# Full 128x128 array tiles for the low key products, the low value products and the meta transposes of a FoX attention

## The chip, the cores and the metric

The kernel runs on one core of one Trainium2 chip, in one launch. The metric is the device time of an execution in microseconds (us). Before the change the median of three runs is 858.16 us (857.74 to 858.84).

## The reference, cut to what matters

One layer of a streaming encoder: a gated linear attention (GLA) and a softmax attention with forget gates (FoX) work on the same normed tokens (512 prompt frames, 16 meta tokens ahead of them, 32 frames of a running stream), and a feed-forward stage follows. The change touches the FoX attention of the prompt, 8 heads of width 64:

```python
def _fox_attend(q, k, v, cq, ck, qpos, kpos):
    s = jnp.einsum('bhqd,bhkd->bhqk', q, k) * (FOX_DH ** -0.5)
    s = s + cq[..., :, None] - ck[..., None, :]           # running sums of log forget gates
    s = jnp.where(kpos[None, :] <= qpos[:, None], s, NEG)
    p = jax.nn.softmax(s, axis=-1)
    return jnp.einsum('bhqk,bhkd->bhqd', p, v)
```

It is called per query block of 128 with all 528 keys (16 meta, 512 prompt); the outputs include the new keys and values, and all of it is float32.

## The kernel before, in words

Every large product is made of three products of split numbers: hi(a)hi(b) + hi(a)lo(b) + lo(a)hi(b), where hi is the value rounded to the matmul type fp32r by ScalarE (ACT) and lo the rest, by VectorE (DVE). A product on TensorE (PE) is a weight load (PEld) of up to 128x128 numbers and a matmul that streams up to 512 columns past them. In the forms of the profile "128\*128" is the array tile: partitions of the contraction \* columns of the weights. "64\*128" uses half of the array's rows, "128\*64" and "128\*16" only some of its columns.

The tokens' projections are computed in units of 128 weight columns: one DMA of 512 KB (`wr`), times the norm's gain on GpSimd (POOL, line 223), split into `wh` and `wl`, then 48 products. In the attention stage, roughly 135 to 295 us of the profiled execution, the small products of the heads stand between these projections as in a zip: `attend()` yields after each small step, and `fill()` then emits 8 products (`GAP_HEAD`) of the next unit in `FILL`: keys (`fk`), queries (`fq`) of a pair of heads, and gates (`ga`, `gb`). The engines run their queues in that order, set at build time.

For each pair of heads `p`, `proj_fk(p)` (line 748) computes the keys `kT` and splits them: `kh` (hi of one head's keys) stands on both halves of the partitions, the second half by a copy on DVE (line 767); lo of both heads goes into columns 1024 to 1551 of the tile `pq`, each head on its own half (line 768). `proj_fq(p)` (line 794) puts into `pq` the queries of each head: hi on the head's own half, lo on the other. So one 128-row product of queries and `kh` gives q·hi(k), and a second one, with the 64 rows of the head's own half, adds hi(q)·lo(k).

`head_scores(h)` (line 902) makes the scores of one head in four query blocks. Its pieces have 144, 272, 400 and 400 + 128 key columns; each is a product with `kh`, one with lo(k), and, but for the first part of the last block, one bf16 product with `mask_b`, all into one PSUM bank. DVE then adds the forget sums and takes the minimum (line 820), ACT takes the exponential (825), DVE normalizes (827, 828). `head_values(h)` (line 924) transposes the probabilities on PE: the 16 meta columns of each query block into `ps_ptm` (line 930), the rest into `ps_pt` (line 940), splits them into `pth` and `ptl`, and multiplies with V. V's tile holds hi(v) in 64 columns and lo(v) in the next 64, so the product with `pth` gives both parts; the one with `ptl` takes the hi columns alone (line 957). The two halves of the result are added at lines 961 and 962.

Of the kernel before, what the change touches and what calls it, by code (L numbers as in the profile page):

```python
# [29 lines left out]
# Token columns: [meta 16 | meta again 16 (unused) | sample 32 | prompt 512].  # L30
TOK = 576
M0 = 32              # first column of the tokens whose outputs are needed
# [6 lines left out]
# Column offsets in w_in.  # L39
GQ, GK, GV, GR, GLR, FQ, FK, FV, FF, GA, GB = 0, 256, 512, 1024, 1536, 1552, 2064, 2576, 3088, 3096, 4120  # L40

# Key columns of the FoX keys: [meta 16 | prompt 512].
KP = META            # first prompt key
# [4 lines left out]
def tile_hybrid_step(  # L48
# [50 lines left out]
    def after(ins, earlier):  # L99
        """order on one engine's queue only"""  # L100
        for e in earlier:
            tc.add_manual_dep(ins, e.name, mybir.DependencyInfo(mybir.DependencyClass.NoSync,
                                                                mybir.DependencyReason.DATA), reason="table")
# [7 lines left out]
    def split_lo(out, in_, hi, eng=None):  # L111
        (eng or DVE).tensor_tensor(out, in_, hi.bitcast(F32), ALU.subtract)  # L112

    # how many products of the projections stand between two steps of a chain of small ones
    GAP_RB, GAP_GATE, GAP_DECAY, GAP_STATE, GAP_OUT, GAP_HEAD, GAP_LEAD = 8, 7, 4, 16, 12, 8, 18

# [9 lines left out]
    # rows 0..16: hi, 32..48: lo, 64..80: hi  # L126
# [23 lines left out]
    # the tensor engine's clock rises with use: some products while the first loads are under way  # L150
# [17 lines left out]
    # suf[t', t] = 1 where t' > t in the same chunk; ind[t', c] = 1 where t' is in chunk c  # L168
    # (ind with zeros on both sides)
# [122 lines left out]
    # hi(x) and lo(x) of the first 64 tokens side by side  # L292
# [27 lines left out]
    def newton(out, y, ms, n, w, name):  # L320
        """out = y * (1.5 - 0.5 * ms * y * y)"""
        a = small([w], name + "_a")
        DVE.tensor_tensor(a[:n], y[:n], y[:n], ALU.mult)
        DVE.scalar_tensor_tensor(a[:n], a[:n], -0.5, ms[:n], ALU.mult, ALU.mult)
        DVE.scalar_tensor_tensor(out, a[:n], 1.5, y[:n], ALU.add, ALU.mult)

    def rsqrt(out, sumsq, n, w, name):
        """out = (sumsq / D + EPS) ** -0.5"""
        ms = small([w], name + "_ms")
        DVE.tensor_scalar(ms[:n], sumsq, 1.0 / D, EPS, ALU.mult, ALU.add)  # L330
        y = small([w], name + "_y")
        ACT.activation(y[:n], ms[:n], AF.Ln)
        ACT.activation(y[:n], y[:n], AF.Exp, scale=-0.5)
        newton(out, y, ms, n, w, name)
# [12 lines left out]
    def token_tile(wh, wl, N, t, ps, kstep=KD):  # L347
        c0, n = TT[t]
        i = 0
        if t == 0:  # L350
            # hi(x) on the first half of the partitions, lo(x) on the second
            for b, k in [(b, k) for k0 in range(0, KD, kstep) for b in (wh, wl) for k in range(k0, k0 + kstep)]:
                mm(ps[:, :N], x2[k // 4][:, k % 4, :], b(k), i == 0, i == 2 * KD - 1)
                i += 1
                yield
            return
        for a, b, k in [(a, b, k) for k0 in range(0, KD, kstep) for a, b in ((xh, wh), (xl, wh), (xh, wl))
                        for k in range(k0, k0 + kstep)]:
            mm(ps[:n, :N], a[:, k, c0: c0 + n], b(k), i == 0, i == 3 * KD - 1)
            i += 1  # L360
            yield
# [75 lines left out]
    # r broadcast over the partitions: rb[p, token] = r[token]  # L437
# [45 lines left out]
    def blocks_steps(key, ks, wh, wl, ah, al, spans, evac, psf, both=False):  # L483
        """out[columns of the weights, tokens]; ah/al(k, a, b) give the moving operand."""
        last = ks[-1]
        pss_ = [psf(f"ps_{key}_{ci}") for ci in range(len(spans))] if both else None
        todo = [(ci, part) for part in (0, 1) for ci in range(len(spans))] if both else \
               [(ci, part) for ci in range(len(spans)) for part in (0, 1)]
        for ci, part in todo:
            a, b = spans[ci]  # L490
            if not both and part == 0:
                ps = psf(f"ps_{key}_{ci}")
            if both:
                ps = pss_[ci]
            i = 0
            for w_, x_ in ((wh, ah), (wl, ah), (wh, al)):
                for k in ks:
                    if (k == last) == bool(part):
                        mm(ps[:, : b - a], w_[:, k, :], x_(k, a, b), part == 0 and i == 0, part == 1 and i == 2)
                        i += 1  # L500
                        yield
            if part:
                evac(ci, a, b, ps[:, : b - a])
# [125 lines left out]
    def evac_fv(t, n, ps):  # L629
# [12 lines left out]
        for g in range(2):  # L642
            src = v[:, 256 * g: 256 * g + 256].rearrange("t (h d) -> t h d", h=4)
            if t == 0:
                # rows 0..15: [hi | lo] against hi(P); rows 32..47: [hi | 0] against lo(P)
                DVE.memset(vt[g].bitcast(F32)[0:48], 0.0)
                ACT.activation(vt[g][0:META, :, 0:64], src[0:META], AF.Copy)
                ACT.activation(vt[g][32:32 + META, :, 0:64], src[0:META], AF.Copy)
                DVE.tensor_tensor(vt[g][0:META, :, 64:128], src[0:META], vt[g][0:META, :, 0:64].bitcast(F32),
                                  ALU.subtract)  # L650
            else:
                ACT.activation(vt[g][:, :, 0:64], src, AF.Copy)
                DVE.tensor_tensor(vt[g][:, :, 64:128], src, vt[g][:, :, 0:64].bitcast(F32), ALU.subtract)
# [6 lines left out]
    # gq into block-diagonal form: per chunk [head 0 tokens | head 1 tokens]  # L660
# [42 lines left out]
    t2 = [blk([TM], F32, f"t2_{hh}", "t2") for hh in range(GH)]  # L703

    def gla_out_steps(name, w, pv, products, dsts):
        """dsts: (tile AP, view of a PSUM-shaped AP) pairs."""
# [37 lines left out]
    kT, pq, kk_, qq_ = [None] * 4, [None] * 4, [None] * 4, [None] * 4  # L744
# [3 lines left out]
    def proj_fk(p):  # L748
# [11 lines left out]
        # hi(k) of a head on both halves of the partitions; lo(k) of both heads  # L760
        pq[p] = ppool.tile([P, PTW], F32R, tag="pt", name=f"pq{p}")
        kk_[p] = [blk([META + SEQ], F32R, f"kh{p}_{hh}") for hh in range(2)]
        for hh in range(2):
# [4 lines left out]
            split_lo(pq[p][own, 1024:1552], k_[own, :], kh[own])  # L768
# [25 lines left out]
    def proj_fq(p):  # L794
# [8 lines left out]
        # hi(q) of a head on its own half of the partitions, lo(q) on the other half  # L803
# [12 lines left out]
    def score_min(sb, a, pv, cb, m, name):  # L816
        """-scores + mask (PSUM) + running sum of log forgets -> sb; running minimum"""
# [30 lines left out]
    def sample_scores(g):  # L848
        """4 heads x 32 queries on the partitions"""
# [44 lines left out]
    # column of (key tile j, query tile i) is 384 j + 128 i  # L894
# [7 lines left out]
    def head_scores(h):  # L902
        p, b0 = h // 2, 64 * (h % 2)
# [3 lines left out]
        for i in range(4):  # L907
            w = META + P * (i + 1)
            q_ = qq_[p][h % 2][:, P * i: P * i + P]
            kh, kl = kk_[p][h % 2], pq[p][b0: b0 + 64, 1024:1552]  # L910
            sb = sbt[:, SBO[i]: SBO[i + 1]]
            m = 3.0e38
            for a, b in ([(0, w)] if i < 3 else [(0, 400), (400, 528)]):
                ps = pss(f"ps_s{h}_{i}_{a}")
                mm(ps[:, 0: b - a], q_, kh[:, a:b], True, False)
                mm(ps[:, 0: b - a], q_[b0: b0 + 64], kl[:, a:b], False, b < w)
# [7 lines left out]
    def head_values(h):  # L924
# [4 lines left out]
        for i in range(4):  # L929
            TE.transpose(pm[:META, P * i: P * i + P], sbt[:, SBO[i]: SBO[i] + META], ident)  # L930
# [24 lines left out]
        for j in range(4):  # L955
            a = 512 * j
            mm(po[0:64, P * j:], V[j + 1][g][:, hh, 0:64], ptl[:, a: a + SEQ - P * j], False, j == 3)
# [92 lines left out]
    # GLA output gate  # L1050
# [68 lines left out]
    # the table of Ln and Exp, back after the last sigmoid  # L1119
# [15 lines left out]
    def final_part(g, tiles, late=None):  # L1135
        """late: what is still to be added to the last block of hs"""
# [18 lines left out]
    def final_early():  # L1155
        """mean of the squares of all but the last block, + EPS"""
# [115 lines left out]
```

## Time and profile before

| | us |
|---|---|
| median of three runs | 858.16 |
| span of the profiled execution, first to last instruction | 855.3 |
| what lies around the span, by the median | 2.9 |
| PE busy, whole span | 837.9 |
| DVE busy, whole span | 450.2 |
| PE busy from 155 to 204 us | 49.0 of 49.0 |
| DVE busy from 204 to 214 us | 9.0 of 10.0 |

PE is busy 98% of the span. But a matmul counts as busy until its modelled end, and matmuls overlap: whether PE could go faster is read from the distance between the starts of consecutive products, not from the busy share. The timeline merges consecutive instructions of one kind into a row with a count (x7). Its second number is from the first one's start to the last one's end.

### The profile page before, as it was taken

Reading aid. Unit: us, or ns where it says so; the run is one execution under the profiler, and the core shown is the slowest. Engines: PE = TensorE matmul, PEld = TensorE weight load, DVE = VectorE, ACT = ScalarE, POOL = GpSimd, SP = SyncE. Lnnn points to the kernel's source line nnn. Section 1 sums busy time; section 2 is a strip of 40 time slices with the busy share of each in tenths; the row PEclk is TensorE's granted clock in tenths of the full one; section 3 lists DMA queues with packets and bytes.
Section 4 is the critical chain, followed back from the end, with each engine's and each line's share of the span. In section 5 each row is a group of like instructions: output and inputs, shape, how many; then the busy total and the mean of one; then the engine's idle time right before and its main releaser. Section 6 shows DMA issues by size and latency. Waiting matters only on the chain.

```text
span 855.3 us, 14966 instructions
## 1 busy us (share of the span) xinstructions
PE 837.9 (98%) x6279; PEld 797.2 (93%) x6279; DVE 450.2 (53%) x828; ACT 311.5 (36%) x567; POOL 159.7 (19%) x162
## 2 busy tenths in 40 slices
PE   8999999999999999999999999999999999999996
PEld 7877898888888999999999999999999999999996
DVE  6765347777657655367576644422333444433434
ACT  6760454454434633222223343411112343411323
POOL 4315111131111376023553000011110000000000
PEclk9997999999999999999999999999999999999999
DMA  8612213421422123323223233223323233223212
GB/s 240 172 49 73 50 43 101 120 77 50 121 57 80 50 74 99 90 84 88 86 79 95 78 95 94 80 74 100 99 77 97 82 91 97 77 74 100 88 37 105
DMA packets 132788, 75.37 MB, mean 88 GB/s; under 512 B 14032, under 2 KB 128000, under 8 KB 132720
## 3 DMA queue, kind: packets, MB, share of 16 engines
q1 hardware_dynamic: 131680, 72.27, 29.7%
q0 software_dynamic: 1024, 2.14, 1.1%
q8 instruction: 49, 0.80, 0.4%
q14 instruction: 19, 0.16, 0.1%
q10 hardware_dynamic: 16, 0.00, 0.0%
HBM read 69.57 MB, written 4.83 MB: 87 GB/s over the span
## 4 chain that ended last, share of the span: by engine, by line
PE 85%; DVE 4%; DMA 3%; POOL 3%; ACT 3%; issue 2%; SPq 0%; ACTq 0%; POOLq 0%; DVEq 0%
PE ps_dn L106 23%; PE ps_up L106 22%; PE ps_ga L106 5%; PE ps_gb L106 5%; PE ps_wo L106 5%; PE ps_fv L106 3%; PE ps_fk L106 3%; PE ps_ya L106 3%; PE ps_yb L106 2%; PE ps_s L106 2%; PE ps_fq L106 2%; DMA wr<-in_w_in_dram 1%; PE ps_pv L106 1%; PE ps_g L106 1%; DVE wl L112 1%
## 5 line engine op out<-in xcount | busy, mean ns | idle before, releaser
L109 ACT ACTIVATE wh<-wr 128x1024 fp32r<-128x1024 f32 x110 | 116.2, 1056 | 273.5 <-PE ps_dn L106 133.2
L112 DVE TENSOR_TENSOR wl<-wr,wh 128x1024 fp32r<-128x1024 f32 x110 | 150.5, 1368 | 99.9 <-ACT wh L109 99.7
L223 POOL TENSOR_TENSOR wr<-wr,gmix 128x1024 f32<-128x1024 f32 x30 | 58.2, 1943 | 149.4 <-DMA wr<-in_w_in_dram 143.1
L106 PE MATMUL ps_up<-xl,wh 128*128 128x256 f32 (+1 forms) x512 | 85.0, 288 | 0.0
L106 PE MATMUL ps_up<-xh,wh 128*128 128x256 f32 (+1 forms) x512 | 85.0, 288 | 0.0
L106 PE MATMUL ps_up<-xh,wl 128*128 128x256 f32 (+1 forms) x512 | 84.9, 288 | 0.0
L106 PE MATMUL ps_dn<-uh,wl 128*128 128x256 f32 (+1 forms) x512 | 80.0, 288 | 0.0
L106 PE MATMUL ps_dn<-uh,wh 128*128 128x256 f32 (+1 forms) x512 | 80.0, 288 | 0.0
L106 PE MATMUL ps_dn<-ul,wh 128*128 128x256 f32 (+1 forms) x512 | 79.7, 287 | 0.0
L1188 DVE SCALAR_TENSOR_TENSOR u<-ps_up,u 128x288 f32<-128x288 f32 x64 | 28.1, 441 | 85.0 <-ACT u L1187 85.0
L106 PEld LDWEIGHTS ps_up<-xh,wh 128*128 128x128 f32 x512 | 72.3, 188 | 0.1
L106 PEld LDWEIGHTS ps_up<-xl,wh 128*128 128x128 f32 x512 | 72.2, 188 | 0.0
L106 PEld LDWEIGHTS ps_up<-xh,wl 128*128 128x128 f32 x512 | 72.0, 188 | 0.0
L106 PEld LDWEIGHTS ps_dn<-uh,wh 128*128 128x128 f32 x512 | 70.5, 188 | 0.0
L106 PEld LDWEIGHTS ps_dn<-uh,wl 128*128 128x128 f32 x512 | 70.2, 188 | 0.0
L106 PEld LDWEIGHTS ps_dn<-ul,wh 128*128 128x128 f32 x512 | 70.0, 188 | 0.0
L1187 ACT ACTIVATE u<-ps_up 128x288 f32<-128x288 f32 x64 | 25.4, 398 | 120.9 <-PE ps_up L106 120.9
L1227 DVE TENSOR_TENSOR dt<-ps_dn,fin 128x288 f32<-128x288 f32 (+1 forms) x32 | 14.1, 441 | 64.2 <-PE ps_dn L106 64.2
L1229 POOL TENSOR_TENSOR xres<-xres,dt 128x288 f32<-128x288 f32 (+1 forms) x16 | 12.4, 776 | 178.2 <-DVE dt L1227 178.2
L825 ACT ACTIVATE sb<-sb,m 128x144 f32<-128x144 f32 (+3 forms) x32 | 18.3, 573 | 34.2 <-DVE m L820 34.2
L106 PE MATMUL ps_ga<-xh,wh 128*128 128x256 f32 (+1 forms) x128 | 22.9, 294 | 1.2 <-DVE qT L798 1.2
L106 PE MATMUL ps_ga<-xh,wl 128*128 128x256 f32 (+1 forms) x128 | 22.5, 295 | 0.5 <-DVE wl L112 0.5
(409 smaller groups left out, 1587.2 us busy)
## 6 DMA issues: line engine op xcount, KB each, us to landing
wr<-in_w_up_dram SPq DMA_DIRECT2D x32, 512.0 KB, 4.0
wr<-in_w_down_dram SPq DMA_DIRECT2D x32, 512.0 KB, 3.9
wr<-in_w_in_dram SPq DMA_DIRECT2D x30, 512.0 KB, 3.9
wr<-in_w_out_dram SPq DMA_DIRECT2D x8, 512.0 KB, 3.8
cb<-cPd SPq DMA_DIRECT2D x8, 264.0 KB, 4.2
x_t<-in_x_prompt_dram SPq DMA_DIRECT2D x4, 512.0 KB, 6.6
gvraw<-in_w_in_dram SPq DMA_DIRECT2D x4, 512.0 KB, 8.7
fvraw<-in_w_in_dram SPq DMA_DIRECT2D x4, 512.0 KB, 3.9
```

The lines of the kernel that those rows point to most:

```text
L106: return TE.matmul(out, lhsT, rhs, start=start, stop=stop, skip_group_check=True)
L109: ACT.activation(out, in_, AF.Copy)
L112: (eng or DVE).tensor_tensor(out, in_, hi.bitcast(F32), ALU.subtract)
L223: POOL.tensor_tensor(raw, raw, gmix.unsqueeze(2).to_broadcast([P, KD, P]), ALU.mult)
L825: exps.append(ACT.activation(sb, sb, AF.Exp, bias=m, scale=-1.0, accum_out=rs).ins)
L1187: ACT.activation(u[:, a:b], ps, AF.Relu)
L1188: DVE.scalar_tensor_tensor(u[:, a:b], ps, 0.0, u[:, a:b], ALU.max, ALU.mult)
L1227: DVE.tensor_tensor(dt_[:, : b - a], ps[:, : b - a], r2[:, a:b], ALU.mult)
L1229: (DVE if hf else POOL).tensor_tensor(hs[d][:, a:b], hs[d][:, a:b], dt_[:, : b - a], ALU.add)
```

## The change

The low part of a head's keys gets a tile of its own, `kl`, from the tag `yf` of the same pool, and a copy on the other half of the partitions as `kh` has; the score product with it uses all 128 rows. As the queries hold hi on one half and lo on the other, this product also adds lo(q)·lo(k). The value product with `ptl` takes all 128 columns of V. The transposes for the meta columns take 128 columns of the probabilities; of what comes out, the first 16 rows are read, as before. The rest of the textual difference is comments that were taken out; line numbers after line 760 shift by up to 3.

```diff
-    kT, pq, kk_, qq_ = [None] * 4, [None] * 4, [None] * 4, [None] * 4
+    kT, pq, kk_, kl_, qq_ = [None] * 4, [None] * 4, [None] * 4, [None] * 4, [None] * 4
...
         kk_[p] = [blk([META + SEQ], F32R, f"kh{p}_{hh}") for hh in range(2)]
+        kl_[p] = [blk([META + SEQ], F32R, f"kl{p}_{hh}", "yf") for hh in range(2)]
         for hh in range(2):
...
             split_hi(kh[own], k_[own, :])
             DVE.tensor_copy(kh[oth], kh[own].bitcast(F32))
-            split_lo(pq[p][own, 1024:1552], k_[own, :], kh[own])
+            kl = kl_[p][hh]
+            split_lo(kl[own], k_[own, :], kh[own])
+            DVE.tensor_copy(kl[oth], kl[own].bitcast(F32))
...
-            kh, kl = kk_[p][h % 2], pq[p][b0: b0 + 64, 1024:1552]
+            kh, kl = kk_[p][h % 2], kl_[p][h % 2]
...
                 mm(ps[:, 0: b - a], q_, kh[:, a:b], True, False)
-                mm(ps[:, 0: b - a], q_[b0: b0 + 64], kl[:, a:b], False, b < w)
+                mm(ps[:, 0: b - a], q_, kl[:, a:b], False, b < w)
...
-            TE.transpose(pm[:META, P * i: P * i + P], sbt[:, SBO[i]: SBO[i] + META], ident)
+            TE.transpose(pm[:, P * i: P * i + P], sbt[:, SBO[i]: SBO[i] + P], ident)
...
-            mm(po[0:64, P * j:], V[j + 1][g][:, hh, 0:64], ptl[:, a: a + SEQ - P * j], False, j == 3)
+            mm(po[:, P * j:], V[j + 1][g][:, hh, :], ptl[:, a: a + SEQ - P * j], False, j == 3)
```

PE's queue before, a piece of 400 columns of the second head between query projections of the second pair (`fq_1`):

```order
L106 MATMUL ps_fq_1_1674<-xh,wl_1503 128x256 x7
L106 MATMUL ps_s_2_0_1695<-kh_1_1395,pq_1393 128x400
L106 MATMUL ps_s_2_0_1695<-pq_1393 128x400
L106 LDWEIGHTS ident_b
L106 MATMUL ps_s_2_0_1695<-mask_b,ident_b 128x128
L106 MATMUL ps_fq_1_1674<-xl,wh_1502 128x256 x7
```

The same place after the change:

```order
L106 MATMUL ps_fq_1_1682<-xh,wl_1507 128x256 x7
L106 MATMUL ps_s_2_0_1703<-kh_1_1395,pq_1393 128x400
L106 MATMUL ps_s_2_0_1703<-kl_1_1397,pq_1393 128x400
L106 LDWEIGHTS ident_b
L106 MATMUL ps_s_2_0_1703<-mask_b,ident_b 128x128
L106 MATMUL ps_fq_1_1682<-xl,wh_1506 128x256 x7
```

No product of PE moves, here or anywhere else, and none is added: 40 score products, 32 value products and 32 transposes change their tile, and nothing else on PE does.

DVE's queue before, where the keys of the second pair are split (`kh_0`, `kh_1` are its two heads, `ptm` and `qT` the meta probabilities of the first head and the queries of the second pair):

```order
L112 TENSOR_TENSOR pq_1612<-kT_1498,kh_0_1613 64x528
L767 CAST kh_1_1614<-kh_1_1614 64x528
L112 TENSOR_TENSOR pq_1612<-kT_1498,kh_1_1614 64x528
L932 TENSOR_TENSOR ptm_1329<-ps_ptm_1644,ptm_1329 16x512
L820 ISA sb_1596,m_1_0_1663<-ps_s_1_0_1659,cb_1594 128x272
L820 ISA m_1_0_1663 128x1
L798 SCALAR_TENSOR_TENSOR qT_1621<-ps_fq_0_1629,rb 128x288
L946 TENSOR_TENSOR ptl_1682<-ps_pt_0_1683,pth_1681 128x128
L800 COPY qS<-qT_1621 128x32
```

DVE's queue there after the change:

```order
L112 TENSOR_TENSOR kl_0_1619<-kT_1502,kh_0_1617 64x528
L768 CAST kh_1_1618<-kh_1_1618 64x528
L771 CAST kl_0_1619<-kl_0_1619 64x528
L112 TENSOR_TENSOR kl_1_1620<-kT_1502,kh_1_1618 64x528
L935 TENSOR_TENSOR ptm_1329<-ps_ptm_1652,ptm_1329 16x512
L771 CAST kl_1_1620<-kl_1_1620 64x528
L823 ISA sb_1600,m_1_0_1671<-ps_s_1_0_1667,cb_1598 128x272
L823 ISA m_1_0_1671 128x1
L801 SCALAR_TENSOR_TENSOR qT_1629<-ps_fq_0_1637,rb 128x288
L949 TENSOR_TENSOR ptl_1690<-ps_pt_0_1691,pth_1689 128x128
L803 COPY qS<-qT_1629 128x32
```

Two copies come in, both ahead of the minimum `m_1_0` and of the evacuation into `qT`. It is so for each of the four pairs; eight copies in all.

## Rows read from the trace of the kernel before

**Rows 1.** Windows: busy us of PE, PEld, DVE, ACT, POOL; granted clock; DMA

```profile
155.00:204.00 49.00, 49.00 (x362) 43.85 (x360) 36.31 (x96) 23.61 (x51) 9.76 (x5) 1.00 0.39 97
278.00:282.40 4.40, 4.40 (x23) 4.09 (x24) 3.73 (x9) 0.80 (x2) 1.75 (x1) 0.61 0.00 0
```

**Rows 2.** Timeline, a projection: start us, us, engine, line, operation, names, tile, shape, count

```profile
144.22 0.99 PEld L106 LDWEIGHTS ps_fq<-xh,wl 128*128 128x128 f32 x7
144.35 1.09 PE L106 MATMUL ps_fq<-xh,wl 128*128 128x288 f32 x7
```

**Rows 3.** Timeline, a score piece of 400 columns with mask

```profile
149.50 0.34 PE L106 MATMUL ps_s<-kh,pq 128*128 128x400 f32 x1
149.77 0.18 PEld L106 LDWEIGHTS ps_s<-pq 64*128 64x128 f32 x1 [0.20 <-issue]
149.77 0.44 PE L106 MATMUL ps_s<-pq 64*128 64x400 f32 x1
150.14 0.10 PEld L106 LDWEIGHTS <-ident_b 128*128 128x128 bf16 x1 [0.19 <-issue]
150.15 0.23 PE L106 MATMUL ps_s<-mask_b,ident_b 128*128 128x128 bf16 x1
...
150.19 1.07 PE L106 MATMUL ps_fq<-xl,wh 128*128 128x256 f32 x7
```

**Rows 4.** Timeline of PE, pieces of 272, of 400 without mask, of 128

```profile
187.04 0.29 PE L106 MATMUL ps_s<-kh,pq 128*128 128x272 f32 x1
...
187.62 0.38 PE L106 MATMUL ps_gb<-xl,wh 128*128 128x288 f32 x1
...
219.35 0.35 PE L106 MATMUL ps_s<-kh,pq 128*128 128x400 f32 x1
...
220.00 0.39 PE L106 MATMUL ps_ga<-xh,wh 128*128 128x256 f32 x1
220.22 0.99 PE L106 MATMUL ps_ga<-xh,wl 128*128 128x256 f32 x7
...
222.32 0.23 PE L106 MATMUL ps_s<-kh,pq 128*128 128x128 f32 x1
...
222.78 0.36 PE L106 MATMUL ps_ga<-xh,wl 128*128 128x256 f32 x1
222.98 0.28 PE L106 MATMUL ps_ga<-xl,wh 128*128 128x256 f32 x1
```

**Rows 5.** Timeline of PE, the value products of one head, then a projection

```profile
204.21 0.84 PE L106 MATMUL ps_pv<-pth,V 128*128 128x512 f32 x4
204.90 0.74 PE L106 MATMUL ps_pv<-ptl,V 128*64 128x512 f32 x4
205.47 0.48 PE L106 MATMUL ps_fq<-xh,wl 128*128 128x288 f32 x2
205.79 0.96 PE L106 MATMUL ps_fq<-xl,wh 128*128 128x288 f32 x6
```

**Rows 6.** Timeline of PE, four meta transposes, and four full ones

```profile
165.15 0.60 PE L930 MATMUL ps_ptm<-ident,sb 128*16 128x128 f32 x4
165.51 0.98 PE L106 MATMUL ps_fk<-xh,wl 128*128 128x320 f32 x5
...
177.20 0.60 PE L940 MATMUL ps_pt<-ident,sb 128*128 128x128 f32 x4
177.56 1.08 PE L106 MATMUL ps_fq<-xh,wh 128*128 128x256 f32 x7
```

**Rows 7.** Groups by line and shape on DVE, 120 to 300 us: busy us, mean ns

```profile
L767 DVE CAST kh<-kh 64x528 fp32r<-64x528 f32 x8 | 3.4, 430 | 0.2
```

**Rows 8.** Timeline, second pair: what held DVE and PE

```profile
150.11 1.90 POOL L223 TENSOR_TENSOR wr<-wr,gmix 128x1024 f32<-128x1024 f32 x1 [9.35 <-DMA wr<-in_w_in_dram]
150.32 1.73 DVE L800 COPY qS<-qT 128x32 f32<-128x32 f32 x1
154.02 1.17 PE L106 MATMUL ps_ga<-xh,wh 128*128 128x288 f32 x7 [0.96 <-DVE qT L798]
```

More of the change, by code (lines that the diff above doesn't have):

```diff
@@ L902, in head_scores @@
     def head_scores(h):
-        p, b0 = h // 2, 64 * (h % 2)
+        p = h // 2
         cb = tmp([META + SEQ], f"cb{h}")
```

## The prediction, made before the changed kernel ran

> **What bounds the kernel now.** I read the page and its table first: PE is busy 98% of the span, so the question is what one of its products costs. Then the windows, for the attention stage, which alone is touched: from 155 to 204 us PE is busy 49.00 of 49.00 us at the full granted clock, while VectorE (DVE) is busy 36.31 [rows 1]. There the end is set by the distances between the starts of PE's products; these I read in the timeline, and at last the places where PE waits for another engine.
>
> *Regular distances.* Where one full-tile product follows another, the next weights load beside the running matmul: seven 128x128 loads take 0.99 us though one takes 0.19, and seven products of 288 columns stand (1.09 - 0.29) / 6 = 0.133 us apart [rows 2]. At 256 columns it is (0.99 - 0.28) / 6 = 0.118 by the row that starts at 220.22 [rows 4]. The slope is 0.015 us per 32 columns; on that line 272 columns make 0.126, 384 make 0.178, 400 make 0.186 and 512 make 0.238 (estimates). Short products cannot go down that line all the way: full transposes, which also load 128 columns and stream 128, start about 0.11 us apart ((0.36 + 0.08) / 4 [rows 6]; the 0.08 is a delay of the next product, explained below). I take 0.11 as the floor for 128 and 144 columns.
>
> *A score piece.* In the piece of 400 columns the product with `kh` starts at 149.50; the weights for the 64-row product are loaded only at 149.77, after 0.20 us in which the load path waits for nothing the profile shows, and the mask product's at 150.14, again after 0.19 [rows 3]. So both ends of the 64-row product are exposed: 0.27 us in place of 0.186 before it, 0.38 after its start. From the first product to the next projection it is 0.69 us, and the seven projections behind take 1.07 where seven regular ones take 0.99 [rows 3, 4]: 0.08 more, 0.77 in all.
>
> **The change part by part.** *Low key products* (40, five per head). If the full tile runs at the regular distance, the 400 piece costs 0.186 + 0.186 + 0.10 for the mask (its load takes 0.10 [rows 3]) = 0.47, not 0.77: gain 0.30. The 272 piece runs 187.04 to 187.62 = 0.58, plus 0.08, against 0.126 + 0.126 + 0.10 = 0.35: gain 0.31. The 400 piece without a mask runs 219.35 to 220.00 = 0.65, and its next product starts 0.22 later, not 0.12: 0.75 against 0.37: gain 0.38. The 128 piece runs 222.32 to 222.78 = 0.46, then 0.20, not 0.12: 0.54 against 0.11 + 0.11 + 0.10 = 0.32: gain 0.22 [rows 3, 4]. The 144 piece I take like the last one. Per head 0.30 + 0.31 + 0.38 + 0.22 + 0.22 = 1.43, times eight heads **11.4 us**.
>
> What no row shows is a bf16 product behind a full fp32r one, since every mask product stands behind a 64-row product now. From below, the mask would cost no more than its streaming, near half of the 0.11 above, say 0.06: 0.04 x 32 = 1.3 us more gain. From above, the wait of 0.2 us ahead of it belongs to the change of type and stays. Then the 32 masked pieces save only what lies between their first two products (0.27 - 0.186 = 0.08 for 400 columns; 0.09 and 0.05 taken for the others by the same reading): 8 x (0.08 + 0.09 + 0.05 + 0.05 + 0.38) = 5.2. I take the first value, because the piece with no mask shows the same 0.37 between start and next load, and no type changes there.
>
> *Low value products* (32). With `pth`, four products of 512, 384, 256 and 128 columns take 204.90 - 204.21 = 0.69; with `ptl` 0.57, and the next two projections 0.32 in place of 2 x 0.133 [rows 5]: 0.69 + 0.57 + 0.05 = 1.31 us. Regular is 2 x (0.238 + 0.178 + 0.118 + 0.11) = 1.29. Gain 0.02 x 8 = **0.2 us**. Bounds: without the floor 1.18 (0.13 x 8 = 1.0 gained); with 64 more columns of load exposed each time, at 0.19 / 128 us per column, 0.095 x 32 = 3.0 lost. The row of `pth`, whose load is full already, is nearest to it, so I stay at 0.2.
>
> *Meta transposes* (32): four of 16 columns take 0.36 to the next projection, four full ones 0.36 as well, both in front of a projection that is as late [rows 6]. Gain 0; the clear bounds are 0.09 each way per head, 0.7 us.
>
> The TensorEngine Tiling (Array Packing) page of the Trainium skill (Key Properties) says that changing the tiling mode drains the array. The 64-row product agrees, with 0.20 us ahead of its load; the 16-column transposes do not, since they cost what full ones do. By the rule these would gain too: eight groups with two changes of about 0.1 each, 1.6 us more.
>
> *Eight copies on DVE*, 0.43 us each [rows 7], 3.4 us. Two per pair of heads come ahead of a minimum and of the evacuation into `qT`. For the first and third pair DVE has idle time behind them or PE has other products; cost 0. In the stretch of the second pair, 144 to 154 us, PE does wait for DVE: 0.96 us for `qT` [rows 8]. But the copy into `qS` ahead of that takes 1.73 for 32 columns, where one of 528 columns takes 0.43 [rows 7, 8], and ends at 152.05, when POOL's 1.90 us product with the gain ends (152.01) [rows 8]. DVE is held there anyway; 0.86 us more ahead of `qS` shortens that hold to 0.87, and the end stays. So the copies cost 0, but in this stretch PE's own gain is lost: three pieces, 0.31 + 0.30 + 0.38 = 1.0 us. The fourth pair repeats the pattern around 209 us with one piece: 0.3. **Lost: 1.3 us.** If a copy starts after POOL instead, it is held itself and pushes all behind it back by up to 1.9 us.
>
> SBUF - State Buffer of the Trainium skill (Who interferes with whom) says that a cast on DVE in a two-port mode and a GpSimd instruction exclude each other, the later one waiting to the end. The length of `qS` agrees; by this rule each of the two stretches has one collision in waiting.
>
> *New waits:* `kl` takes tiles that the value weights held, done before; sums and pair outputs that use the same tiles later come when the scores of that pair are over. PE's and SP's queues wait for nothing new of note.
>
> **Sum.** 11.4 + 0.2 - 1.3 = 10.3 us off the profiled execution's span of 855.3, so 845.0; with the 2.9 us around it, which bring the span to the median of 858.16, **847.9 us**.
>
> **Rivals.** *Mask keeps the wait:* 5.2 + 0.2 - 1.3 = 4.1, so 854.1. For it: the mask's load waits 0.19 us today. Against: the piece without a mask waits as long.
>
> *DVE takes it back:* in both stretches a copy meets POOL, 2 x 1.9 = 3.8 lost, 851.7. For it: `qS` shows the hold, and the last copy would begin about 0.3 us ahead of POOL (an estimate, from durations). Against: POOL starts by a DMA that DVE's own split of the weights releases, so both move together. With the mask rival as well, 857.9.
>
> *Slower: the load is not hidden.* The weights of the low product could wait for the product before because both use the same rows and the same queries, whatever the tile. Then pieces stay at 0.77 us, the longer loads cost up to 3.0 us in the value products, and two collided stretches cost up to 3.8: 858.2 + 3.0 + 3.8 = 865, or 861.2 with the loads alone. It decides as soon as the score pieces gain less than what these cost. Against it: full loads overlap running products on the same 128 rows everywhere else [rows 2].
>
> TensorE: Matmul & The Clock Gate of the Trainium skill (Part 3, The mechanism) says that a load overlaps a running matmul only where the row groups differ; by it this rival would be the outcome. Rows 2 contradict it for full tiles.
>
> *More than the sum:* from 278.0 to 282.4 us the granted clock is 0.61, partly the 1.2 GHz level [rows 1], after a stretch of short products. If that goes, seven of its products no longer take double: some 1.7 us, 846.2; the tiling page's 1.6 us for the meta transposes end at the same place. The clock could as well fall for longer there, as PE arrives earlier and waits for the softmax.
>
> The change does not do all that its name says: the 48-row product with the meta probabilities stays a partial tile; its exposed time stays, and none of the sums counts it.
>
> **How the numbers follow.** Forecast 0.64; mask 0.13; DVE 0.11; both 0.02; slower 0.04; more than the sum 0.06. The range reaches from 844.2 (mask at 0.06, 1.3; value products at their bound, 0.8; part of the clock) to 854.0, where the mask rival ends. Below 0.2% (1.7 us), which is about what a measurement can tell from none, lie the joint rival and a little of the edges of others: same 0.03; slower 0.04; faster 0.93.
>
> **What would show it.** `ps_s` rows of 128\*128 on `kl`, the second product 0.18 us after the first at 400 columns, and the mask's load with no idle time ahead of it. If the mask's load still waits 0.19 us, the second case holds; if the low product's own load waits, the slower one. The `qS` copies should be near 0.9 us in the second and fourth pair; a copy of `kl` of 1 us or more there shows the collision. `ps_pv` and the meta groups should look as before. The forecast is wrong if the attention stage does not end some 10 us earlier, or if stages behind it change.

## The result, and the profile after

The median is 846.65 us (842.91 to 846.83, four runs), against 857.95 us (855.55 to 858.84, four runs) of the kernel before beside it: a ratio of 0.9868, with an interval of 0.9837 to 0.9899. The forecast was 847.9 us and "faster". The profiled execution took 846.64 us, its span 844.9 us, 10.4 us less than before. Beside the later kernels below, the kernel before had medians of 854.75 to 855.70 us, so the 11.3 us between the two medians here are at the upper end.

The span moves with the clock of stages that the change does not touch. Before, the granted clock was at half for parts of 74 to 85 us; after, for parts of 74 to 81 us. (It also fell at the very end, from 852 us before and from 839 us after, but there PE has no product left.) So I compare the attention stage by itself, from the start of the first `ps_fk` to the start of the last row of value products with `ptl`, both read in PE's timeline. It ran from 118.84 to 293.57 us before (174.73 us) and from 118.04 to 283.39 us after (165.35 us): 9.4 us shorter. What follows takes 561.7 us before and 561.5 us after. The other 0.8 us lies ahead of the stage, where the dip of the clock was shorter. Each length is that of one profiled execution; how far it varies between executions was not measured.

The score piece of 400 columns with mask, after (timeline; PE with one row of PEld), answers to [rows 3]:

```profile
147.72 0.34 PE L106 MATMUL ps_s<-kh,pq 128*128 128x400 f32 x1
147.90 0.35 PE L106 MATMUL ps_s<-kl,pq 128*128 128x400 f32 x1
148.08 0.10 PEld L106 LDWEIGHTS <-ident_b 128*128 128x128 bf16 x1 [0.17 <-issue]
148.08 0.23 PE L106 MATMUL ps_s<-mask_b,ident_b 128*128 128x128 bf16 x1
148.12 0.96 PE L106 MATMUL ps_fq<-xl,wh 128*128 128x256 f32 x6
```

The reader is to see the distances between starts: 0.18 and 0.18 us where [rows 3] have 0.27 and 0.38, and 0.04 behind the mask. The load path still idles 0.17 us ahead of the mask's load, but the mask's product comes at the distance that 400 columns take anyway. The last row is cut off by the view's window: all seven projections take 1.08 us, as late as before (1.07). The other pieces, to be held against [rows 4]:

```profile
183.75 0.29 PE L106 MATMUL ps_s<-kh,pq 128*128 128x272 f32 x1
...
184.04 0.38 PE L106 MATMUL ps_gb<-xl,wh 128*128 128x288 f32 x1
...
215.34 0.34 PE L106 MATMUL ps_s<-kh,pq 128*128 128x400 f32 x1
...
215.70 0.28 PE L106 MATMUL ps_ga<-xh,wh 128*128 128x256 f32 x1
215.82 1.00 PE L106 MATMUL ps_ga<-xh,wl 128*128 128x256 f32 x7
...
217.94 0.23 PE L106 MATMUL ps_s<-kh,pq 128*128 128x128 f32 x1
218.00 0.28 PE L106 MATMUL ps_s<-kl,pq 128*128 128x128 f32 x1
...
218.16 0.36 PE L106 MATMUL ps_ga<-xh,wl 128*128 128x256 f32 x1
218.36 0.28 PE L106 MATMUL ps_ga<-xl,wh 128*128 128x256 f32 x1
```

The 272 piece takes 0.29 us, not 0.58; the one with no mask 0.48 to the second projection, not 0.87; the 128 piece 0.42 to the second projection, not 0.66.

The value products (timeline of PE, after; [rows 5]):

```profile
199.53 0.84 PE L106 MATMUL ps_pv<-pth,V 128*128 128x512 f32 x4
200.22 0.81 PE L106 MATMUL ps_pv<-ptl,V 128*128 128x512 f32 x4
200.87 0.48 PE L106 MATMUL ps_fq<-xh,wl 128*128 128x288 f32 x2
201.19 0.69 PE L106 MATMUL ps_fq<-xl,wh 128*128 128x288 f32 x4
```

With `ptl` it is now 0.65 us where it was 0.57; the two projections behind take 0.32 as before. Six of the eight heads lose 0.05 to 0.08 us in this way; in the last two, where projections stand between the two groups, it stays at 0.58 to 0.59. In all that is 0.4 us. The meta transposes stay at 0.35.

What PE waited for (view of waits; us in total, times, longest), first before, from 118 to 295 us, then after, from 118 to 284 us:

```profile
PE ps_ga L106 <- DVE qT L798: 1.2, 2, 1.0
PE ps_s L106 <- DVE pq L112: 0.8, 1, 0.8
```

```profile
PE ps_ga L106 <- ACT sb L828: 1.6, 1, 1.6
PE ps_ga L106 <- DVE qT L801: 1.0, 1, 1.0
PE ps_s L106 <- DVE pq L112: 0.7, 1, 0.7
PE ps_s L106 <- DVE m L823: 0.6, 1, 0.6
PE ps_fk L106 <- DVE qT L801: 0.2, 1, 0.2
```

2.0 us of waits became 4.1. Three of the rows are in the second pair (152 us, 1.6), the fourth (209 us, 1.0) and at 141 us (0.6). Two of the places (timeline, after; [rows 8]):

```profile
138.31 2.06 DVE L831 TENSOR_SCALAR sb<-sb,ri 128x272 f32<-128x272 f32 x1
138.32 1.90 POOL L223 TENSOR_TENSOR wr<-wr,gmix 128x1024 f32<-128x1024 f32 x1 [5.40 <-DMA wr<-in_w_in_dram]
...
149.15 1.90 POOL L223 TENSOR_TENSOR wr<-wr,gmix 128x1024 f32<-128x1024 f32 x1 [8.94 <-DMA wr<-in_w_in_dram]
150.13 0.95 DVE L803 COPY qS<-qT 128x32 f32<-128x32 f32 x1
152.38 0.91 PE L106 MATMUL ps_ga<-xh,wh 128*128 128x288 f32 x5 [1.57 <-ACT sb L828]
```

The copy into `qS` still ends with POOL, and takes 0.95 instead of 1.73 us, near the 0.9 forecast; PE, which arrives earlier, waits longer behind it. At 138 us a scaling of the probabilities now meets POOL in full; before, one at the same place took 1.09. The eight copies of `kl` took 430 ns each, as [rows 7].

The products that ran under the clock of 0.61 before ([rows 1]), from the transposes at 278.81 us on, start at 270.21 us after the change, and the clock is whole there (windows; the clock is the third number from the end):

```profile
270.00:272.00 2.00, 2.00 (x17) 1.92 (x18) 1.43 (x7) 0.49 (x1) 1.81 (x1) 1.00 0.00 0
```

That this dip went is not shown to be the change's doing: e2, e4 and e10 below keep 64-row score products and do not have it either. Without its 1.7 us the stage before is 173.0 us long, and the change gains 7.7.

So the stage's account is: 11.4 us gained at the score pieces and 1.7 at the clock, 0.4 lost at the value products; 12.7. As 9.4 came, about 3.3 us went into waits of PE for DVE and ACT. The view of waits shows 2.1 us of it as idle time; by the distances between starts, 0.8 are at 141 us, 0.8 more than before in the fourth pair and 0.7 in the second, and the rest are gaps of 0.3 us and less.

### The profile page after: what moved, and what is told of

The parts are those of the page before. It is cut to its first block, busy times and chain, and to the rows that moved or that the text cites. A ratio compares the mean times of both kernels' runs of the same rounds, so it can differ in the third digit from the quotient of the medians.

```text
span 844.9 us, 14973 instructions
## 1 busy us (share of the span) xinstructions
PE 824.1 (98%) x6279; PEld 793.3 (94%) x6279; DVE 451.0 (53%) x836; ACT 311.2 (37%) x567; POOL 159.7 (19%) x162
## 3 DMA queue, kind: packets, MB, share of 16 engines
q0 software_dynamic: 1024, 2.14, 1.1%
## 4 chain that ended last, share of the span: by engine, by line
PE 83%; DVE 5%; DMA 3%; ACT 3%; POOL 3%; issue 2%; SPq 0%; ACTq 0%; POOLq 0%; DVEq 0%
PE ps_up L106 23%; PE ps_dn L106 23%; PE ps_gb L106 5%; PE ps_ga L106 5%; PE ps_wo L106 5%; PE ps_fv L106 3%; PE ps_ya L106 3%; PE ps_yb L106 3%; PE ps_fk L106 2%; PE ps_fq L106 2%; DMA wr<-in_w_in_dram 1%; DVE wl L112 1%; PE ps_s L106 1%; PE ps_g L106 1%; PE ps_pv L106 1%
## 5 line engine op out<-in xcount | busy, mean ns | idle before, releaser
L106 PE MATMUL ps_gb<-xh,wl 128*128 128x256 f32 (+1 forms) x128 | 22.8, 294 | 0.2 <-DVE wl L112 0.2
```

Of the source, the lines that this page charges most:

```text
L106: return TE.matmul(out, lhsT, rhs, start=start, stop=stop, skip_group_check=True)
```

## The experiments

The ratios are to the kernel before run beside each; "stage" is the length defined above, of one profiled execution; "waits" the sum of PE's waits in that view over the stage.

| kernel | median us (runs) | ratio, interval | stage us | waits us |
|---|---|---|---|---|
| before (profiled) | 857.95 (4) | | 174.73 | 2.0 |
| after (profiled) | 846.65 (4) | 0.9868, 0.9837–0.9899 | 165.35 | 4.1 |
| e1_keys_only | 847.35 (4) | 0.9893, 0.9875–0.9912 | 165.27 | 4.5 |
| e2_values_meta_only | 856.56 (10) | 1.0023, 0.9999–1.0046 | 174.01 | 2.0 |
| e3_zero_halves | 847.09 (4) | 0.9896, 0.9861–0.9931 | 168.67 | 4.8 |
| e4_both64 | 849.44 (1) | | 173.27 | 1.5 |
| e5_full48 | 841.80 (4) | 0.9838, 0.9800–0.9876 | 163.30 | 4.7 |
| e8_qs_psum | 846.33 (4) | 0.9873, 0.9819–0.9928 | 164.99 | 3.5 |
| e9_nogain_after | 838.14 (1) | | 161.64 | 1.3 |
| e10_nogain_before | 847.96 (1) | | 170.91 | 0.0 |
| e11_keys48qs | 843.40 (6) | 0.9856, 0.9819–0.9893 | 163.23 | 4.6 |
| e13_keys48qs_tt | 844.69 (6) | 0.9874, 0.9840–0.9909 | 163.67 | 4.5 |
| e14_keys48qs_act | 842.76 (6) | 0.9858, 0.9825–0.9892 | 161.12 | 2.7 |

**The score products alone** (e1: the two other edits undone in the kernel after).

```diff
-            TE.transpose(pm[:, P * i: P * i + P], sbt[:, SBO[i]: SBO[i] + P], ident)
+            TE.transpose(pm[:META, P * i: P * i + P], sbt[:, SBO[i]: SBO[i] + META], ident)
...
-            mm(po[:, P * j:], V[j + 1][g][:, hh, :], ptl[:, a: a + SEQ - P * j], False, j == 3)
+            mm(po[0:64, P * j:], V[j + 1][g][:, hh, 0:64], ptl[:, a: a + SEQ - P * j], False, j == 3)
```

> The changed kernel with the low value products and the meta transposes put back to their partial tiles; only the low key products are full. Theory (the gain lies in the score pieces, 11.4 us; the full low value products take 0.65 us per head in place of 0.57 to 0.59): about 0.5 us less than the changed kernel, span near 844.4, the rows of ps_pv on ptl back at 0.57 to 0.59, pieces as in the changed kernel (0.41, 0.37, 0.30, 0.22 from the first product to the next projection). Rival (every change of tile costs about 0.1 us, the narrow ones too): 1.6 us or more slower than the changed kernel, span 846.5 or above.

The stage is 165.27 us, that of the full change, with pieces at the same distances and the products with `ptl` back at 0.57 to 0.59 us; a wait of 0.8 us near the end (behind an operation of DVE) hides the 0.4 us that these give back. The score products carry the whole gain.

**The value products and transposes alone** (e2: the same lines the other way round, in the kernel before).

> The kernel before with only the low value products and the meta transposes on full tiles; the low key products stay on 64 rows. Theory: within 0.6 us of the kernel before, rather above it (eight heads by 0.06 us for the full low value products), ps_ptm groups at 0.36 as before. Rival (changes to and from narrow tiles cost too): 1.6 to 2.4 us faster than before.

A ratio of 1.0023, with 1 inside the interval. Four products with `ptl` take 0.63 to 0.65 us in the first six heads, the transposes 0.35. The stage, 174.01 us, has no dip of the clock, so it is 1.0 us longer than the one before without its dip (173.0); 0.4 of that are the value products, and the rest is not assigned. A tile with few columns (16 or 64) costs nothing here to enter or leave; filling it costs the value products 0.05 to 0.08 us in those six heads.

**No copies on DVE** (e3: the other half of `kl` is set to zero, by POOL ahead of the stage, instead of copied; lo(q)·lo(k) is left out, as in the kernel before).

```diff
+            POOL.memset(kl_[p][hh].bitcast(F32)[64 - 64 * hh: 128 - 64 * hh], 0.0)
...
-            DVE.tensor_copy(kl[oth], kl[own].bitcast(F32))
```

> The changed kernel, but the other half of each kl tile is zeroed by GpSimd before it is needed instead of copied by DVE; the eight copies are gone, and the product adds q times zero there. Theory (DVE's eight copies lengthen the two stretches in which PE waits for DVE): PE's waits in the second and the fourth pair, 1.7 and 1.2 us in the changed kernel, fall to about what they were before the change (1.2 and 0.4), 1.3 us less, and the span to about 843.5. Rival (the copies are hidden in what GpSimd holds of DVE, and the waits grew because PE arrives earlier): waits and span as in the changed kernel within 0.4 us.

The copies are gone and the waits are not less: 4.8 us. The second pair (timeline):

```profile
144.18 1.90 POOL L223 TENSOR_TENSOR wr<-wr,gmix 128x1024 f32<-128x1024 f32 x1 [8.64 <-DVE m L824]
144.53 1.58 DVE L804 COPY qS<-qT 128x32 f32<-128x32 f32 x1
...
148.08 1.17 PE L106 MATMUL ps_ga<-xh,wh 128*128 128x288 f32 x7 [1.96 <-DVE qT L802]
```

Without the copies `qS` starts earlier against POOL and is held for longer: 1.58 us, to POOL's end again. That shows the forecast's cover. After PE's idle stretch the clock fell (windows):

```profile
146.00:148.00 2.00, 0.12 (x1) 0.00 (x0) 1.49 (x8) 1.31 (x4) 0.07 (x1) 1.00 0.00 0
148.00:150.00 2.00, 1.92 (x13) 1.96 (x14) 2.00 (x5) 1.95 (x4) 0.00 (x0) 0.88 0.00 0
150.00:152.00 2.00, 2.00 (x12) 2.00 (x10) 1.94 (x5) 0.81 (x2) 0.00 (x0) 0.50 0.29 66
152.00:154.00 2.00, 2.00 (x15) 2.00 (x14) 1.16 (x5) 0.83 (x2) 0.00 (x0) 0.77 0.64 143
```

That is 1.7 us of full clock lost, and as much again at 206 to 212 us, in the fourth pair. The stage is 168.67 us long; without these 3.4 us it would be 165.3, as in the kernel after. So the rival's account holds for the copies: they cost nothing that this run shows.

**Both products on 64 rows** (e4: the kernel before with lo(q)·hi(k) left out).

```diff
-                mm(ps[:, 0: b - a], q_, kh[:, a:b], True, False)
+                mm(ps[:, 0: b - a], q_[b0: b0 + 64], kh[b0: b0 + 64, a:b], True, False)
```

> The kernel before with both score products on the head's own 64 rows, so lo(q) times hi(k) is left out. Theory (the exposed time belongs to the change between a 128-row and a 64-row tile): the second product of a 400 column piece starts 0.18 to 0.19 us after the first with no idle time ahead of its load; the first product's load now waits about 0.2 us for the projection before it, the mask's load still 0.19; the piece takes about as long as before, 0.77 us with the delays around it, and the span stays within 2 us of 855.3. Rival (a load of 64 rows always waits for the product before it, whatever its tile): 0.38 us between the two products, the piece 0.2 us longer or more, the span 6 us longer.

A piece of 400 columns (timeline, PE and two loads):

```profile
184.74 0.52 PE L106 MATMUL ps_gb<-xl,wh 128*128 128x256 f32 x3
185.19 0.45 PE L106 MATMUL ps_s<-kh,pq 64*128 64x400 f32 x1
...
185.30 0.19 PEld L106 LDWEIGHTS ps_s<-pq 64*128 64x128 f32 x1
185.48 0.34 PE L106 MATMUL ps_s<-pq 64*128 64x400 f32 x1
185.75 0.10 PEld L106 LDWEIGHTS <-ident_b 128*128 128x128 bf16 x1 [0.27 <-issue]
185.75 0.23 PE L106 MATMUL ps_s<-mask_b,ident_b 128*128 128x128 bf16 x1
185.79 0.36 PE L106 MATMUL ps_gb<-xl,wh 128*128 128x256 f32 x1
```

Behind the first 64-row product the second one's load runs after 0.11 us, beside it. The first product comes 0.09 us late: three projections of 256 columns take 0.45 us to it, not 3 x 0.118 = 0.35. But the second starts 0.29 us behind the first, not the 0.18 to 0.19 of the expectation, and the mask's product 0.27 behind the second, where full tiles have 0.18. The piece itself takes 0.60 us, with the entry 0.70, as much as before (0.69). The stage agrees: 173.27 us, without a dip of the clock, against 173.0. So two 64-row products in a row pay once what one pays, about 0.28 us; of that, 0.09 stand at the entry, 0.11 between the two and 0.08 behind them. That all of it hangs on the change of rows is therefore not shown: why 0.11 us stand between two products on the same rows stays open. The run also weakens the rival that the same queries or rows made the load wait.

**The last product on part of the rows** (e5: `ptm` and its V with 128 rows, zero from 48 on).

```diff
-            mm(po, V[0][g][0:48, hh, :], ptm[0:48, :], True, False)
+            mm(po, V[0][g][:, hh, :], ptm, True, False)
```

> The kernel after the change, and in addition the value product with the meta probabilities, which still uses 48 of the 128 rows, gets all 128: the rows from 48 on are zero on both sides, set once. Theory (what a product pays is the change of the number of rows in use, once before it and once behind it): in the kernel after, this product starts about 0.10 us later than the regular distance, and the next one 0.42 us behind it, where 512 columns make 0.238. So 0.10 + 0.18 = 0.28 us a head, 8 heads 2.2 us: the distance behind it falls from 0.42 to 0.24 and the attention stage gets 2.2 us shorter. Rival (0.42 is the price of loading weights for a product whose data ptm were just written, or of a new accumulation): the distance stays 0.42 and the stage too.

Timeline of PE, first the kernel after, then this one:

```profile
222.41 0.99 PE L106 MATMUL ps_gb<-xh,wh 128*128 128x256 f32 x7
223.33 0.49 PE L106 MATMUL ps_pv<-ptm,V 48*128 48x512 f32 x1
223.75 0.85 PE L106 MATMUL ps_pv<-pth,V 128*128 128x512 f32 x4
224.44 0.81 PE L106 MATMUL ps_pv<-ptl,V 128*128 128x512 f32 x4
```

```profile
219.45 0.99 PE L106 MATMUL ps_gb<-xh,wh 128*128 128x256 f32 x7
220.28 0.39 PE L106 MATMUL ps_pv<-ptm,V 128*128 128x512 f32 x1
220.51 0.75 PE L106 MATMUL ps_pv<-pth,V 128*128 128x512 f32 x4
221.10 0.80 PE L106 MATMUL ps_pv<-ptl,V 128*128 128x512 f32 x4
```

From the projections to `ptl` 2.03 us became 1.65: 0.09 before the product, 0.19 behind it, 0.10 in the group with `pth`, whose first product had carried a delay I had taken for regular. That is 0.38 us in five of the eight heads; the others gain less, as delays behind the product grow, and the distances around the value products sum to some 2.5 us over the stage. The stage gained 2.05, as a wait for DVE of 0.8 us came in at 177 us. The price of rows is the same for 48 as for 64 (0.09 ahead, 0.19 behind), and here nothing but the rows changed, no tile was added; the expectation was low by a quarter (0.28 of 0.38) for a head, and left the growing waits out.

**`qS` straight from PSUM** (e8).

```diff
-                DVE.tensor_copy(qS[:, p, :], q_[:, 0:SMP])
+                DVE.scalar_tensor_tensor(qS[:, p, :], ps[:, 0:SMP], -0.125, rb[:, a:a + SMP], ALU.mult, ALU.mult)
```

> The kernel after the change, in which the 32 sample columns of the queries are written into qS straight from PSUM, by the same kind of operation as qT, and no longer copied from qT in SBUF. Theory (POOL's product with the gain holds a DVE copy within SBUF but no operation that reads PSUM): the operation takes about 0.2 us also in the second and fourth pair, where the copy took 0.95 and 0.72; what stands behind it on DVE comes 0.75 and 0.5 us earlier, and PE's waits of 1.72 us behind the scores of the second pair and of 1.21 us in the fourth shrink by about as much: stage 1.0 to 1.3 us shorter. Rival: the next operation of DVE within SBUF (the scaling of sb) is held in its place until POOL ends, or the softmax's chain of minimum, exponential and reciprocal sets the end anyway: no gain, waits as in the kernel after.

In the second pair (timeline):

```profile
149.10 2.00 POOL L223 TENSOR_TENSOR wr<-wr,gmix 128x1024 f32<-128x1024 f32 x1 [8.71 <-DMA wr<-in_w_in_dram]
150.10 0.18 DVE L803 SCALAR_TENSOR_TENSOR qS<-ps_fq,rb 128x32 f32<-128x32 f32 x1
```

0.18 us in the middle of POOL's product. PE's delays shrink from 1.72 to 1.19 us in the second pair and from 1.21 to 0.56 in the fourth. Yet the stage is only 0.4 us shorter, not 1.0 to 1.3: at 268.89 us a scaling of `sb` took 2.14 us beside POOL, which began at 268.91, and PE waited 0.8 there. Both theories had a part: the copy was held, and elsewhere another operation was.

**No product of POOL in the stage's first 16 units** (e9 and e10: the norm's gain is left out for them, in the kernel after and before).

```diff
-        if parts[0].shape[0] == D and key[0] in IN_KEYS:
+        if parts[0].shape[0] == D and key[0] in IN_KEYS and key not in FILL:
```

> The kernel after the change, in which POOL's product with the norm's gain is left out for the 16 weight units of the attention stage, so that POOL does nothing beside DVE there. Theory A (the gain that is missing, about 3.2 us of waits for DVE, comes from POOL holding DVE's copies and scalings while PE arrives earlier): no operation of DVE takes over 1 us but the long splits, the waits of 0.77 us at 141, 1.72 at 150 and 1.21 at 208 us fall to a third or less, and the stage, 165.35 us, loses 2 us or more. Theory B (the chain of the softmax, from scores over minimum, exponential and reciprocal back to the queue of DVE, sets the end in these places): the waits stay within 0.3 us of what they were.

> The kernel before the change with the same product of POOL left out for the 16 weight units of the attention stage. Theory A (POOL's hold): its waits, 1.0 us at 134, 1.23 at 154 and 0.38 at 209, fall by up to 1.5 us together, less than in the kernel after, so that the two stages without POOL's product are 10.9 us apart (11.4 less 0.5 of the low value products), but for a dip of the granted clock in either. Theory B (softmax's chain): both fall alike, and the distance stays near 9.4, or 7.7 without the dip of the clock at 278 us.

PE's waits of e9 (e10 has none):

```profile
PE ps_pt L943 <- DVE yfs L893: 0.8, 1, 0.8
PE ps_ga L106 <- ACT sb L828: 0.5, 1, 0.5
```

After the change 3.7 us of the stage go with POOL's product, before it 3.8, of which 1.7 are the dip of the clock at 278 us that e10 does not have: 2.1. The first wait of e9 stands beside POOL's product for a later unit, which is left (five of them run from 225 us on); a scaling beside it takes 2.06 us. The second is in the second pair, where POOL now does nothing: of the 1.72 us there 0.70 stay, which speaks for theory B, the softmax's chain, in that place. The stages are 170.91 - 161.64 = 9.27 us apart; e9's two delays between products, 1.00 and 0.70 us, have no counterpart in e10: 10.97, against the 11.4 - 0.4 = 11.0 of the products alone. So of the 3.3 us that the change did not bring, 1.6 (3.7 - 2.1) are shown to be POOL's hold on DVE; 1.0 stands beside a product of POOL that was left, and is put down to the same hold without a run that takes it away; 0.7 is left where POOL is idle.

**Putting it together** (e11: e1, e5 and the edit of `qS` in one kernel).

> What the runs so far point to, put together: full tiles for the low key products and for the product with the meta probabilities, the 64-column value products and 16-column transposes of before, and qS straight from PSUM. Theory (only the number of rows in use costs; columns do not; DVE held by POOL takes back part): stage 163.3 us of the full 48-row kernel, less 0.5 us for the value products and up to 1.2 for qS: 161.6 to 162.8 us. Time by the profiled execution's dips of the clock between 838 and 844 us. Rival (PE now waits for DVE wherever it gains): the stage stays at 163.3 or above.

The stage is 163.23 us, as that of e5: the rival is right. The longer hold is again another operation's: seven scalings meet POOL and take 1.35 us or more, the longest, 2.11 us, in the tail, where PE waits 1.2 us.

**The scaling as a product of two tensors** (e13: e11 with another operation).

```diff
-        DVE.tensor_scalar(sb, sb, ri, None, ALU.mult)
+        DVE.tensor_tensor(sb, sb, ri.to_broadcast([sb.shape[0], sb.shape[1]]), ALU.mult)
```

> The kernel of the same submission, in which DVE scales the probabilities by a product of two tensors (sb and ri, broadcast) instead of a product with a scalar per partition. Theory (of DVE's operations within SBUF only those that run at two elements a cycle are held by POOL, as copies and scalings; products of two tensors, at 1.3 ns per element in the splits, are not): no scaling over 0.75 us, where single ones now take 2.06; each costs its plain excess, 0.1 to 0.25 us by 144 to 528 columns, 32 of them some 5 us of DVE's idle time; PE's waits in the second and fourth pair and in the tail fall below 0.5 us each; stage about 161 us. Rival (the scaling stands in the softmax's chain, so each excess is paid by PE where it waits for DVE): stage as in the other kernel or up to 2 us longer.

The theory failed, and the stage is 163.67 us, as the rival had it (timeline):

```profile
134.76 1.90 POOL L223 TENSOR_TENSOR wr<-wr,gmix 128x1024 f32<-128x1024 f32 x1 [5.12 <-DVE ri L830]
135.03 1.92 DVE L831 TENSOR_TENSOR sb<-sb,ri 128x272 f32<-128x272 f32 x1
```

A product of two tensors in SBUF is held too: it ends 0.29 us behind POOL's. So the speed of the operation does not decide; copies, scalings and two-tensor products within SBUF were all held, and the operation that reads PSUM (e8) was not. SBUF - State Buffer of the Trainium skill (Who interferes with whom) says of products of two tensors that with both inputs in SBUF they contend with GpSimd's reads. The 1.92 us agree.

**The scaling on ScalarE** (e14: e11 with it on ACT).

```diff
-        DVE.tensor_scalar(sb, sb, ri, None, ALU.mult)
+        ACT.activation(sb, sb, AF.Copy, scale=ri)
```

> Like e11_keys48qs, but the probabilities are scaled by ScalarE (ACT), which is busy 84.75 of 163 us there, and not by DVE. Theory (the holds of DVE's scalings by POOL, eight of them with 9 us in excess in the stage of e11, set PE's waits): without them DVE holds none but splits and copies; ACT gets 32 operations of some 0.3 to 0.6 us; PE's waits at the places of 140, 151, 179, 205, 208 and 269 us of e11 (together some 5 us) fall to 2 us or less, stage 160 to 161 us instead of 163.23. Rival (each scaling now waits in ACT's queue for DVE's reciprocal, behind and ahead of exponentials and splits of weights, so the softmax's chain gets longer): stage 163 us or above.

The stage is 161.12 us, 4.2 less than in the kernel after, and PE's waits are 2.7. Its time does not show that: ahead of the stage the clock fell at 7 to 11 and at 72 to 83 us in this profiled execution, and not while PE worked in that of e5; what lies around the stage took 679.6 us in e14 and 676.7 in e5. By time, e5, e11 and e14 (ratios 0.9838, 0.9856, 0.9858) cannot be told from each other, nor surely from the change itself (0.9868).

## Why the prediction was right, point by point

- **Score pieces, 11.4 us.** Right in mechanism and sum. By the rows the pieces gain 0.29 (400), 0.29 (272), 0.39 (no mask) and 0.24 (128); the 144 piece went from 0.47 to 0.22 us with 0.08 behind both: 0.25. That is 1.46 a head, 11.7 us; e9 and e10 put it at 10.97 + 0.4 = 11.4. Two parts of it were off, by little: 0.11 us is no floor for short products (`kh` to `kl` takes 0.06 at 128 columns), and the mask costs 0.04 with the delay of 0.08 still behind it, not 0.10.
- **The mask rival** fell, but the sign that I named for it did not tell: the idle 0.17 us ahead of the mask's load is there and costs nothing at 400 columns. The distance between the products is what tells.
- **Value products, +0.2 us:** wrong in sign, 0.4 us lost, inside the bounds of +1.0 and -3.0. I laid the regular line against the row with `pth`, which held a delay of the 48-row product ahead of it, as e5 shows.
- **Meta transposes, 0:** right (e2). TensorEngine Tiling (Array Packing) of the Trainium skill (Key Properties) says that changing the tiling mode drains the array; of the narrow tiles here the trace agrees for 64 and 48 rows, with 0.09 us ahead and 0.19 us behind, and not for 16 or 64 columns.
- **Copies at 0:** right, and by the cover named: `qS` ends with POOL, with them (0.95 us) and without them (1.58 us). The *DVE* rival fell by little: the last copy in the second pair began at 148.74 us, 0.41 us ahead of POOL's product.
- **"Lost: 1.3 us"** is the step that was mis-sized: it is 3.3. I priced only the gain of PE's own pieces in two stretches. But a PE that is early shifts DVE's work against POOL's products, and the scaling at 138 us met one in full (2.06 us, excess 1.7); there and in the fourth pair waits grew that I had counted at 0 and 0.3, by 0.8 each. DVE was not held for longer in all: over what they take undisturbed, the held scalings and `qS` copies took about 8.9 us before and 6.9 after (an estimate from the durations in the two timelines). Without POOL's product the kernel before gains 2.1 us and the one after 3.7, so the same kind of hold costs an earlier PE more.
- **The clock at 278 us**, a rival at 0.06, went, and gave back its 1.7 us. The forecast span of 845.0 against 844.9 is therefore luck in part: 2.0 us more waits and 0.6 at the value products were met by 1.7 at the clock, 0.8 ahead of the stage and 0.2 behind it, none of which the forecast counted. At a whole clock the stage gained 7.7 us where 10.3 were forecast. Nearly all of the 1.3 us by which 847.9 missed the median is another term: 2.9 us were added around the span, and in the profiled execution after it is 1.7 (846.64 - 844.9).

What stays open is when the clock falls. Ahead of the stage its dips differ between the profiled executions, and the stage starts between 112.5 and 119.1 us; that they also make the spread of the four runs after the change (842.91 to 846.83 us) is likely but not shown, and none of these runs varied their cause. What follows the stage takes 561.3 to 562.1 us in all of them.

## What to carry to other kernels

Price a product on part of the array's rows by the distances around it, entry and exit both, and fill the rows with zeros or a copy where nothing else is late; narrow columns may stay. When PE gets faster by spots, look for operations within SBUF on DVE that can meet a long one on GpSimd, and move them to PSUM operands (0.4 us here) or to ScalarE (2.1 us, e11 to e14) first. Where dips of the clock are as large as the effect, compare the length of the stage in the traces, less the dips that fall inside it, and two kernels without the suspected hold, rather than totals. A dip in which PE has no work costs nothing: each execution has one at its end, of different length, and what follows the stage takes the same within 0.8 us.

## What was not expected of the hardware

- A product of 128 columns can follow one with other moving data after 0.06 us, though its own load takes 0.19: `kl` at 218.00 us, behind `kh` at 217.94.
- DVE's copies (1.73 us for 32 columns), scalings (2.14) and two-tensor operations (1.92) within SBUF ended with POOL's 1.90 us product or up to 0.3 us behind it; operations that read PSUM (0.18) were not held, nor the reciprocal of 128x1 (0.17 at 150.50 us in e8, beside POOL).
- Two 64-row products in a row are 0.29 us apart at 400 columns, full tiles 0.18 (e4).
- Two microseconds in which PE was busy for 0.12 were followed by six at 0.88, 0.50 and 0.77 of the clock (e3): 1.7 us of full clock. The 0.50 is the lower of its two levels, 1.2 of 2.4 GHz.
